# Fourier branch of a two-layer diffusion backbone: the short transform's PSUM tile moves to the single ring, and 16 convolution taps per layer move from the branch's end into the gates

## The chip, the core and the metric

The kernel runs on one core of one Trainium2 chip. Its engines are TensorE (PE; its weight loads PEld), VectorE (DVE), ScalarE (ACT), GpSimd (POOL) and SyncE (SP), which issues the transfers. The metric is the device time of one execution in microseconds. The kernel before takes 2163.43 us, the median of three runs (2162.35 to 2165.26).

## The reference

Two layers are applied to 640 tokens (512 of a sample, 128 of a prompt) of width 1024. What matters here are the three parallel mixers of a layer, their gates and the merge:

```python
f_in, conv_in, q_lat, kv_lat, k_rope = jnp.split(u, cuts, axis=-1)
y_f = fourier_mix(f_in) @ W['w_fourier'][l]
y_c = conv_module(conv_in, ...)      # gate, 31 taps, layer_norm, silu, matmul
y_a = block_attention(q, k, v) @ W['w_mla_out'][l]
gates = jax.nn.sigmoid(h @ W['w_gate'][l] + W['b_gate'][l])
gf, gc, ga = jnp.split(gates, N_BRANCH, axis=-1)
x = x + g1 * ((gf * y_f + gc * y_c + ga * y_a) @ W['w_out'][l])

def fourier_mix(f_in):               # (B, L, 512), 4 groups of 128 channels
    z = f_in.astype(jnp.float32).reshape(B, L, F_GROUPS, F_GROUP_W)
    y = jnp.fft.fft2(z, axes=(1, 3), norm='ortho').real
    return y.reshape(B, L, F_W).astype(f_in.dtype)

def layer_norm(x, g, b):             # over the 512 convolution channels
    mu = jnp.mean(xf, axis=-1, keepdims=True)
    var = jnp.mean(jnp.square(xf - mu), axis=-1, keepdims=True)
    y = (xf - mu) * lax.rsqrt(var + EPS)
```

The Fourier transform runs over the tokens too: over 512 for the sample, over 128 for the prompt.

## The kernel before

Channels lie on the partitions and the 640 tokens along the free dimension, in two halves of 320. Every large product is made of three (L621, `mm3`): a weight is cut into a high part `whi` (ScalarE, L182) and a low part `wlo` (VectorE, L183), the activation likewise (`split`, L666 and L667), and high by high, high by low and low by high are added up in PSUM. Weights come in one planned stream of DMAs (`Stream`), are split two pieces ahead of their use, and sit in small rings of buffers.

PSUM has two rings: `psum()` (`ps`) gives three tiles of two banks each, `psum1()` (`ps1`) two tiles of one bank. The next user of a tile waits on TensorE until the last readers of its former content are done.

After the attention, `mixers` runs: the Fourier branch (`fourier`), eight gates `gf` (each `gate`: eight blocks of the gate's weights, 48 matmuls, then four blocks of the branch's output weights, 24 matmuls), eight gates `ga` for the attention, eight `gc` for the convolution, and the output projection. In `fourier` four products give `fT` (L1265), five channel transforms of 128 tokens each give `Th`, `Tl` and `tp` (L1284), the long transform over 512 tokens fills two `ps` tiles (L1313 to L1320), and for each of two pairs of groups the short one over 128 tokens fills `pq` (L1326 to L1328): its cosine part in the first bank, its sine part in the second (column 512). ScalarE copies the cosine part (L1334), VectorE takes difference and sum with the sine part (L1335, L1336), ScalarE mirrors the halves (L1338, L1339) and the results are split into `yh` and `yl`, which the gates `gf` read.

The convolution is a generator, `conv_gen`, that other code steps through `fill(n)`. Its 124 taps (L1105, L1107) are VectorE work, one step each. Step 125 adds the four accumulators up (`cs`, L1116), sums them over the channels with a matmul by ones (`colsum`, L491) and takes the mean on ScalarE (L1120). Step 126 subtracts the mean (L1123), squares and adds (`sumsq`, L500 to L504, result `sqa`), sums `sqa` over the channels with L491 again, and forms the inverse deviation (L454 to L458). Steps 127 to 130 finish one channel block each. The order in the program is the order of these calls; the framework then moves single instructions forward on an engine where they are ready, so that taps of two blocks alternate on VectorE. Each engine works through its own list in order.

Of the kernel before, what the change touches and what calls it, by code (L numbers as in the profile page):

```python
# [14 lines left out]
ALU = mybir.AluOpType  # L15
# [190 lines left out]
class Kern:  # L206
# [936 lines left out]
    def mixers(self, l, h, oT, xsrc, up, upp, uctx, wctx):  # L1143
        nc, tc = self.nc, self.tc
# [3 lines left out]
        with self.rpool("mix") as mp, ExitStack() as ctx:  # L1148
# [3 lines left out]
            def b640(n):  # L1152
                return [r640("b", F32R, 16) for _ in range(n)]
# [5 lines left out]
            def fill(n):  # L1159
                for _ in range(n):  # L1160
                    next(bg, None)
# [4 lines left out]
            with self.rpool("m1") as lp:  # L1166
                ad = self.ada_gate() if l == 0 else iter(())
                m1 = [lp.tile([128, NT], F32, tag="m1", name=self.nm("m1"), bufs=8) for _ in range(8)]
                for m in range(8):
                    self.gate(l, r640, "gf", "wf", m, hh, hl, yh, yl, bgh[:, m : m + 1], m1[m])  # L1170
                    next(ad, None)
                    fill(9)
                next(ad, None)
                oh, ol = b640(4), b640(4)
                for k in range(4):
                    self.split(oh[k], ol[k], oT[k])
                x = []
                for k in range(KT):
                    t = self.xt()
                    nc.sync.dma_start(out=t, in_=xsrc[:, k, :])  # L1180
                    x.append(t)
                self.x = x
                for m in range(8):
                    t = self.gate(l, r640, "ga", "wa", m, hh, hl, oh, ol, bgh[:, 16 + m : 17 + m], None)
                    nc.vector.tensor_tensor(m1[m], m1[m], t, op=ALU.add)
                    fill(7)
                for _ in bg:
                    pass
                ctx.close()
                uctx.close()  # L1190
                actx = ExitStack()
                ad = iter(())
                if l == 0:
                    ad = self.ada_dots(actx.enter_context(self.lpool("ad")), [(0, 24, 40)])
                with self.rpool("mm") as mm:
                    mh, ml = [], []
                    for m in range(8):
                        mh += b640(1)
                        ml.append(mm.tile([128, NT], F32R, tag="ml", name=self.nm("ml"), bufs=8))
                        t = self.gate(l, r640, "gc", "wc", m, hh, hl, U[0], U[1], bgh[:, 8 + m : 9 + m], None)  # L1200
                        nc.vector.tensor_tensor(m1[m], m1[m], t, op=ALU.add)
                        r = self.split(mh[m], ml[m], m1[m])
                        with tc.issue_after(r.ins):
                            for _ in range(1 + m % 2):
                                next(ad, None)
                    g1h = self.lay.tile([128, 8, 2], F32, tag="g1h", name=self.nm("g1h"))
                    nc.vector.tensor_scalar(g1h, self.mods[l][:, 16:24, :], 0.5, None, op0=ALU.mult)
                    segs = (((0, 0, 320, 0),), ((0, 320, 192, 0), (192, 512, 128, 1)))
                    cols = ((0, 320), (320, 640))
                    nm = self.norm_gen(  # L1210
                        l, 2, lambda n: lp.tile([128, NT], F32, tag="m1", name=self.nm(n), bufs=8)
                    )
                    next(nm)
                    for m in range(6):
                        p = self.psum()
                        q = (p[:, 0:320], p[:, 512:832])
                        self.gemm(p, l, "wo", m, mh, ml)
                        for b in range(2):
                            r = self.addx(m, q[b], g1h, segs[b])
                        with tc.issue_after(r.ins):  # L1220
                            next(ad, None)
                        if m == 3:
                            for _ in ad:
                                pass
                            actx.close()
                            wx = wctx.enter_context(self.lpool("wx"))
                        next(nm)
                    w = [[self.st.get("wo", l, m, h) for h in range(2)] for m in (6, 7)]

                    def run(i, k):  # L1230
                        c = slice((k % 4) * 128, (k % 4 + 1) * 128)
                        wh, wl = w[i][k // 4]
                        return lambda oo: self.mm3(oo, wh[:, c], wl[:, c], mh[k], ml[k], k == 0, k == 7)

                    self.st.spare["upa", l, 1] = (wx, "f")
                    return self.last_pair(nm, [[run(i, k) for k in range(8)] for i in range(2)], cols, segs, g1h, 6)
# [24 lines left out]
    def fourier(self, l, fo, hh, hl, yh, yl, r640, fill):  # L1261
        nc = self.nc
        fT = []
        for m in range(4):
            p = self.psum()  # L1265
            self.gemm(p, l, "f", m, hh, hl)
            t = fo.tile([128, NT], F32, tag="fT", name=self.nm("fT"), bufs=4)
            nc.scalar.copy(self.halves(t), self.v2(p))
            fT.append(t)
            fill(5)  # L1270
        Th, Tl = [], []

        def tview(t):
# [6 lines left out]
        for i in range(5):  # L1280
            p = self.psum()
            for g in range(4):
                o = (g // 2) * 512 + (g % 2) * 130
# [3 lines left out]
            if i < 4:  # L1287
                a = fo.tile([128, 520], F32R, tag="Th", name=self.nm("Th"), bufs=4)
                b = fo.tile([128, 520], F32R, tag="Tl", name=self.nm("Tl"), bufs=4)
# [3 lines left out]
            else:  # L1293
                tp = fo.tile([128, 520], F32, tag="tp", name=self.nm("tp"))
                nc.scalar.copy(tview(tp), pview(p))

        def wcols(t, pr, kind):
            o, n = {"P": (0, 128), "Q": (128, 128), "K": (256, 2)}[kind]
            return t[:, pr * 260 + o : pr * 260 + o + n]

        ps = [self.psum() for _ in range(2)]
# [19 lines left out]
                                    ps[pr][:, 0:258], lhsT=wcols(a[i], pr, "P"), rhs=b[:, r], start=first, stop=fin  # L1321
                                )
        for pr in range(2):
            pq = self.psum()
            Cp, Sp = self.tb[:, 130:196], self.tb[:, 196:262]
            nc.tensor.matmul(pq[:, 0:66], lhsT=wcols(tp, pr, "P"), rhs=Cp, start=True, stop=True)  # L1326
            nc.tensor.matmul(pq[:, 512:578], lhsT=wcols(tp, pr, "Q"), rhs=Sp, start=True, stop=True)
            nc.tensor.matmul(pq[0:2, 512:578], lhsT=wcols(tp, pr, "K"), rhs=Cp, start=False, stop=True, skip_group_check=True)  # L1328
            ym = self.xt(name="ym")
            yp = self.xt(name="yp")  # L1330
            for src, o, L in ((ps[pr], 0, 512), (pq, 512, 128)):
                hw = L // 2 + 1
                pc = r640("gt", F32, 2)
                nc.scalar.copy(pc[:, 0:hw], src[:, 0:hw])  # L1334
                nc.vector.tensor_tensor(ym[:, o : o + hw], pc[:, 0:hw], src[:, 512 : 512 + hw], op=ALU.subtract)  # L1335
                nc.vector.tensor_tensor(yp[:, o : o + hw], pc[:, 0:hw], src[:, 512 : 512 + hw], op=ALU.add)  # L1336
                for d, s in ((ym, yp), (yp, ym)):
                    nc.scalar.copy(d[:, o + hw : o + L], s[:, o + hw - 2 : o : -1])  # L1338
                    nc.scalar.copy(d[0:2, o + hw : o + L], d[0:2, o + hw - 2 : o : -1])  # L1339
            self.split(yh[2 * pr], yl[2 * pr], ym)  # L1340
            self.split(yh[2 * pr + 1], yl[2 * pr + 1], yp)
            fill(6)
    def ffn(self, l, h2):
        nc = self.nc
        hh, hl = h2
# [281 lines left out]
```

## Time and profile before

| | |
|---|---|
| Median of three runs | 2163.43 us |
| The profiled execution | 2164.37 us |
| Its span, first to last instruction | 2162.6 us |
| Mean granted clock of TensorE | 0.996 |
| TensorE, VectorE, ScalarE busy | 2119.4, 1499.8, 916.0 us |

The profile names each instruction by its line and by what it writes and reads (`out<-in`). A row of the timeline gives its start, its time and in brackets how long the engine stood idle before it and what it waited for by the profile. Matmuls overlap: a row's time is longer than the step from one to the next. A wait for several engines is put down to the one that came last by the profile, and that can be the wrong one. The clock of TensorE has two levels, 1.2 and 2.4 GHz, shown as 0.50 and 1.00.

### The profile page before, as it was taken

The numbers are of one execution on the slowest core, as the hardware profiler recorded it, in microseconds if no ns is written. First come the engines' busy times: TensorE is split into PE (matmuls) and PEld (weight loads), VectorE is DVE, ScalarE is ACT, GpSimd is POOL, SyncE is SP. The second block draws the span as 40 slices with busy tenths as digits, with TensorE's granted clock in tenths as the row PEclk, the third lists the DMA queues.
The fourth block names the chain that finished last, engine by engine and source line by source line (L and its number), as shares of the span: only waits on it lengthen the run. The fifth ranks groups of instructions, "written<-read, shape, count | busy, mean of one in ns | idle before, by whom it ended". The sixth has DMA issues, their size and how long they took to land.

```text
span 2162.6 us, 35613 instructions
## 1 busy us (share of the span) xinstructions
PE 2119.4 (98%) x14380; PEld 2046.3 (95%) x14380; DVE 1499.8 (69%) x2585; ACT 916.0 (42%) x1786; POOL 115.7 (5%) x243
## 2 busy tenths in 40 slices
PE   6999999999999999999999999999999999999999
PEld 4988899999999999999988889999999999999998
DVE  6675699757778868977877767996544864455454
ACT  4654342353345424514456553424432643343242
POOL 0242100000000000000002421000000000000000
PEclk9999999999999999999999999999999999999999
DMA  7211033324424344444431101222222222222222
GB/s 279 64 50 30 30 104 124 110 98 147 156 88 136 128 156 137 152 151 132 154 104 61 44 21 50 93 93 73 78 75 78 69 76 72 79 79 69 78 74 79
DMA packets 61797, 209.32 MB, mean 97 GB/s; under 512 B 7488, under 2 KB 8512, under 8 KB 61376
## 3 DMA queue, kind: packets, MB, share of 16 engines
q1 hardware_dynamic: 61632, 207.04, 29.2%
q8 instruction: 113, 1.85, 0.4%
q14 instruction: 52, 0.43, 0.1%
HBM read 201.47 MB, written 5.54 MB: 96 GB/s over the span
## 4 chain that ended last, share of the span: by engine, by line
PE 64%; DVE 3%; ACT 1%; POOL 1%; issue 0%; DMA 0%; DVEq 0%; ACTq 0%; POOLq 0%
PE ps L621 60%; PE ps L953 1%; PE ps L1007 1%; DVE wlo L183 1%; PE ps L990 1%; PE ps L827 0%; DVE hl L552 0%; PE ps L936 0%; DVE nt L548 0%; DVE cacc L1107 0%; PE ps L847 0%; ACT P L941 0%; ACT whi L182 0%; PE ps L994 0%; PE ps L593 0%
## 5 line engine op out<-in xcount | busy, mean ns | idle before, releaser
L182 ACT CAST whi<-raw 128x512 fp32r<-128x512 f32 (+3 forms) x546 | 332.4, 611 | 872.2 <-PE ps L621 807.3
L621 PE MATMUL ps<-hh,whi 128*128 128x320 f32 x2720 | 641.2, 313 | 10.5 <-ACT hh L551 3.7
L621 PE MATMUL ps<-hh,wlo 128*128 128x320 f32 x2720 | 640.5, 311 | 4.4 <-DVE wlo L183 4.4
L621 PE MATMUL ps<-hl,whi 128*128 128x320 f32 x2720 | 640.1, 311 | 0.8 <-DVE hl L552 0.4
L183 DVE TENSOR_TENSOR wlo<-raw,whi 128x512 fp32r<-128x512 f32 (+3 forms) x544 | 370.6, 688 | 235.2 <-ACT whi L182 231.9
L621 PEld LDWEIGHTS ps<-hh,whi 128*128 128x128 f32 x2720 | 457.8, 189 | 19.5 <-ACT hh L551 5.6
L621 PEld LDWEIGHTS ps<-hh,wlo 128*128 128x128 f32 x2720 | 460.4, 189 | 6.4 <-DVE wlo L183 5.9
L621 PEld LDWEIGHTS ps<-hl,whi 128*128 128x128 f32 x2720 | 461.2, 189 | 5.3 <-DVE hl L552 3.7
L621 PE MATMUL ps<-b,whi 128*128 128x320 f32 x1024 | 207.1, 308 | 0.0
L1107 DVE SCALAR_TENSOR_TENSOR cacc<-up,cdwh,cacc 128x656 f32<-128x656 f32 x240 | 206.4, 901 | 0.7
L1381 DVE SCALAR_TENSOR_TENSOR ft<-fr,pf,ft 128x641 f32<-128x641 f32 x176 | 155.3, 885 | 57.4 <-ACT ft L1377 56.2
L322 DVE SCALAR_TENSOR_TENSOR junk<-adw,cb 128x1024 f32<-128x1024 f32 x144 | 175.7, 1220 | 1.0 <-DMA adw<-in_adt 0.9
L621 PE MATMUL ps<-al,whi 128*128 128x320 f32 x704 | 165.3, 310 | 0.0
L621 PE MATMUL ps<-ah,whi 128*128 128x320 f32 x704 | 165.2, 309 | 0.1
L621 PEld LDWEIGHTS ps<-b,whi 128*128 128x128 f32 x1024 | 164.8, 188 | 0.0
L621 PE MATMUL ps<-ah,wlo 128*128 128x320 f32 x704 | 164.2, 309 | 0.0
L621 PE MATMUL ps<-b,wlo 128*128 128x320 f32 x640 | 151.3, 309 | 0.0
L621 PEld LDWEIGHTS ps<-ah,whi 128*128 128x128 f32 x704 | 118.8, 188 | 1.6 <-ACT ah L666 1.6
L621 PEld LDWEIGHTS ps<-al,whi 128*128 128x128 f32 x704 | 118.5, 188 | 0.6
L621 PEld LDWEIGHTS ps<-ah,wlo 128*128 128x128 f32 x704 | 118.6, 188 | 0.1
L1241 DVE SCALAR_TENSOR_TENSOR x<-ps,g2h,x 128x320 f32<-128x320 f32 (+1 forms) x144 | 54.8, 435 | 83.9 <-PE ps L621 83.7
L621 PEld LDWEIGHTS ps<-b,wlo 128*128 128x128 f32 x640 | 108.2, 188 | 0.2
(272 smaller groups left out, 2258.9 us busy)
## 6 DMA issues: line engine op xcount, KB each, us to landing
raw<-in_ws SPq DMA_DIRECT2D x247, 512.0 KB, 3.4
adw<-in_adt SPq DMA_DIRECT2D x72, 512.0 KB, 4.2
ad<-in_ad SPq DMA_DIRECT2D x16, 512.0 KB, 9.9
raw<-in_ws SPq DMA_DIRECT2D x20, 384.0 KB, 3.1
x<-in_xT SPq DMA_DIRECT2D x16, 320.0 KB, 4.0
xd<-x SPq DMA_DIRECT2D x8, 320.0 KB, 2.6
x<-xd SPq DMA_DIRECT2D x8, 320.0 KB, 3.1
out_yT<-x SPq DMA_DIRECT2D x8, 320.0 KB, 2.2
```

Of the source, the lines that this page charges most:

```text
L182: nc.scalar.copy(h, src)
L183: nc.vector.tensor_tensor(l, src, h.bitcast(F32), op=ALU.subtract)
L322: nc.vector.scalar_tensor_tensor(junk, w[at(n)], 0.5, cb[:, v], op0=ALU.mult, op1=ALU.mult, accum_out=md[:, i, v : v + 1])
L621: nc.tensor.matmul(o, lhsT=w, rhs=x[:, lo:hi], start=(start and i == 0), stop=(stop and i == 2))
L953: nc.tensor.matmul(p[:, c * 512 : c * 512 + 320], lhsT=a[:, i * 128 : (i + 1) * 128], rhs=b[:, c * 320 : c * 320 + 320], start=(n == 0), s ...
L990: nc.tensor.transpose(p[:, b * 128 : (b + 1) * 128], src[:, b * 128 : (b + 1) * 128], self.ident)
L1007: nc.tensor.matmul(p[n * 64 : (n + 1) * 64, 0:256], lhsT=vv[b][:, 2 * j + n, :], rhs=pts[j, h][:, b, n, :], start=(b == 0), stop=(b == 4),)
L1107: nc.vector.scalar_tensor_tensor(a, up[m][:, t : t + UCW], ws, a, op0=ALU.mult, op1=ALU.add)
L1241: r = self.nc.vector.scalar_tensor_tensor(xs, p[:, pc : pc + n], g[:, m, v : v + 1], xs, op0=ALU.mult, op1=ALU.add)
L1381: nc.vector.scalar_tensor_tensor(t[:, c], raw[:, o : o + 641], w[:, 3 * jj + tap : 3 * jj + tap + 1], t[:, c], op0=ALU.mult, op1=ALU.add,)
```

## The change

Two things are edited. The short transform's tile `pq` comes from `psum1()`, so both parts lie in one bank, the sine part from column 256. And `fill` is called with other counts: in `fourier` behind the fourth product 0 instead of 5 and behind the third 4; behind the pairs 0 and 2 instead of 6 and 6; in the gates `ga` 8 instead of 7.

```diff
@@ mixers, the gates ga
                     nc.vector.tensor_tensor(m1[m], m1[m], t, op=ALU.add)
-                    fill(7)
+                    fill(8)
@@ fourier
             fT.append(t)
-            fill(5)
+            fill((5, 5, 4, 0)[m])
...
         for pr in range(2):
-            pq = self.psum()
+            pq = self.psum1()
             Cp, Sp = self.tb[:, 130:196], self.tb[:, 196:262]
             nc.tensor.matmul(pq[:, 0:66], lhsT=wcols(tp, pr, "P"), rhs=Cp, start=True, stop=True)
-            nc.tensor.matmul(pq[:, 512:578], lhsT=wcols(tp, pr, "Q"), rhs=Sp, start=True, stop=True)
-            nc.tensor.matmul(pq[0:2, 512:578], lhsT=wcols(tp, pr, "K"), rhs=Cp, start=False, stop=True, skip_group_check=True)
+            nc.tensor.matmul(pq[:, 256:322], lhsT=wcols(tp, pr, "Q"), rhs=Sp, start=True, stop=True)
+            nc.tensor.matmul(pq[0:2, 256:322], lhsT=wcols(tp, pr, "K"), rhs=Cp, start=False, stop=True, skip_group_check=True)
...
-            for src, o, L in ((ps[pr], 0, 512), (pq, 512, 128)):
+            for src, o, L, b in ((ps[pr], 0, 512, 512), (pq, 512, 128, 256)):
...
-                nc.vector.tensor_tensor(ym[:, o : o + hw], pc[:, 0:hw], src[:, 512 : 512 + hw], op=ALU.subtract)
-                nc.vector.tensor_tensor(yp[:, o : o + hw], pc[:, 0:hw], src[:, 512 : 512 + hw], op=ALU.add)
+                nc.vector.tensor_tensor(ym[:, o : o + hw], pc[:, 0:hw], src[:, b : b + hw], op=ALU.subtract)
+                nc.vector.tensor_tensor(yp[:, o : o + hw], pc[:, 0:hw], src[:, b : b + hw], op=ALU.add)
...
-            fill(6)
+            fill((0, 2)[pr])
```

The first place is TensorE at the end of layer 1's Fourier branch, where the first gate follows the short transform. The name before the first number is the ring, the first number the tile. Before:

```order
L1326 MATMUL ps_1626_14673<-tb_103,tp_1623_14577 128x66
L1327 MATMUL ps_1626_14673<-tb_103,tp_1623_14577 128x66
L1328 MATMUL ps_1626_14673<-tb_103,tp_1623_14577 2x66
L1326 MATMUL ps_1631_14705<-tb_103,tp_1623_14577 128x66
L1327 MATMUL ps_1631_14705<-tb_103,tp_1623_14577 128x66
L1328 MATMUL ps_1631_14705<-tb_103,tp_1623_14577 2x66
L621 MATMUL ps_1646_14750<-hh_1087_11430,whi330_14627 128x320 x2
L621 MATMUL ps_1646_14750<-hl_1095_11438,whi330_14627 128x320 x2
```

In the changed kernel:

```order
L1326 MATMUL ps1_1626_14667<-tb_103,tp_1623_14571 128x66
L1327 MATMUL ps1_1626_14667<-tb_103,tp_1623_14571 128x66
L1328 MATMUL ps1_1626_14667<-tb_103,tp_1623_14571 2x66
L1326 MATMUL ps1_1631_14693<-tb_103,tp_1623_14571 128x66
L1327 MATMUL ps1_1631_14693<-tb_103,tp_1623_14571 128x66
L1328 MATMUL ps1_1631_14693<-tb_103,tp_1623_14571 2x66
L621 MATMUL ps_1645_14733<-hh_1087_11430,whi330_14621 128x320 x2
L621 MATMUL ps_1645_14733<-hl_1095_11438,whi330_14621 128x320 x2
```

The instructions and their sequence are the same. The short transform's two tiles are of the ring `ps1`, and in the ring `ps` the gate's tile (1645) follows those of the long transform (1624 and 1625, on L1313 to L1320).

The second place is TensorE in layer 1's gates `ga`, at the two column sums of the convolution. Before, with the gate between them cut out:

```order
L621 MATMUL ps_15853<-b_15563,wlo_15794 128x320 x2
L491 MATMUL ps_15894<-cs_15890,ones 128x328 x2
L621 MATMUL ps_15899<-hh_11430,whi_15823 128x320 x2
...
L621 MATMUL ps_15960<-b_15563,wlo_15903 128x320 x2
L491 MATMUL ps_16008<-sqa_15997,ones 128x328 x2
L621 MATMUL ps_16057<-hh_11430,whi_15930 128x320 x2
```

In the changed kernel:

```order
L621 MATMUL ps_16041<-b_15550,whi_15981 128x320 x2
L621 MATMUL ps_16041<-b_15546,wlo_15982 128x320 x2
L491 MATMUL ps_16080<-cs_16076,ones 128x328 x2
L491 MATMUL ps_16100<-sqa_16089,ones 128x328 x2
L621 MATMUL ps_16131<-hh_11430,whi_16011 128x320 x2
L621 MATMUL ps_16131<-hl_11438,whi_16011 128x320 x2
```

The two sums stood before and behind the fourth gate; now they stand one behind the other, behind the fifth gate. Layer 0 has the same.

The third place is VectorE at those sums, from the merge of the gate's result (L1185) on. Before:

```order
L1185 TENSOR_TENSOR m_1640_14744<-m_1640_14744,gt_15851 128x640
L1123 TENSOR_TENSOR cacc_14332<-cacc_14332,cmu_15897 128x656
L1123 TENSOR_TENSOR cacc_14736<-cacc_14736,cmu_15897 128x656
L1123 TENSOR_TENSOR cacc_15148<-cacc_15148,cmu_15897 128x656
L1123 TENSOR_TENSOR cacc_15455<-cacc_15455,cmu_15897 128x656
L183 TENSOR_TENSOR wlo_15964<-raw_15961,whi_15963 128x512
L504 TENSOR_TENSOR sqa_15997<-sqa_15997,sq_15999 128x656
L504 TENSOR_TENSOR sqa_15997<-sqa_15997,sq_16002 128x656
L504 TENSOR_TENSOR sqa_15997<-sqa_15997,sq_16005 128x656
L183 TENSOR_TENSOR wlo_16059<-raw_15961,whi_16058 128x512
```

In the changed kernel:

```order
L1185 TENSOR_TENSOR m_1641_14729<-m_1641_14729,gt_16039 128x640
L1123 TENSOR_TENSOR cacc_14332<-cacc_14332,cmu_16083 128x656
L1123 TENSOR_TENSOR cacc_14932<-cacc_14932,cmu_16083 128x656
L1123 TENSOR_TENSOR cacc_15332<-cacc_15332,cmu_16083 128x656
L1123 TENSOR_TENSOR cacc_15672<-cacc_15672,cmu_16083 128x656
L504 TENSOR_TENSOR sqa_16089<-sqa_16089,sq_16091 128x656
L504 TENSOR_TENSOR sqa_16089<-sqa_16089,sq_16094 128x656
L504 TENSOR_TENSOR sqa_16089<-sqa_16089,sq_16097 128x656
L456 SCALAR_TENSOR_TENSOR rt_16105<-rs_16104 128x656
L457 SCALAR_TENSOR_TENSOR rt_16105<-ps_16100,rt_16105 128x656
L458 SCALAR_TENSOR_TENSOR rs_16104<-rt_16105,rs_16104 128x656
```

The weight split between the subtractions (L1123) and the additions (L504) has gone, as have a split and the next gate's product (L1256) and merge (L1185) between the additions and the work on the inverse deviation (L456 to L458).

## Rows read from the trace of the kernel before

**Rows 1.** Page, part 1: busy us (share of the span) and instructions of each engine.

```profile
PE 2119.4 (98%) x14380; PEld 2046.3 (95%) x14380; DVE 1499.8 (69%) x2585; ACT 916.0 (42%) x1786; POOL 115.7 (5%) x243
```

**Rows 2.** Waits of TensorE: who waits, for whom: us, times, longest.

```profile
PE ps L537 <- DVE sqa L504: 13.7, 1, 13.7
PE ps L621 <- DVE wlo L183: 4.4, 4, 3.6
...
PE ps L621 <- ACT yp L1338: 1.7, 1, 1.7
```

**Rows 3.** Timeline, TensorE, layer 1's Fourier end: start, us, operation, xcount [idle <- releaser].

```profile
1372.67 0.28 PE L1328 MATMUL ps<-tb,tp 128*2 128x66 f32 x2
1374.60 0.87 PE L621 MATMUL ps<-hh,whi 128*128 128x320 f32 x2 [1.65 <-ACT yp L1338]
```

**Rows 4.** Timeline, VectorE, the same place.

```profile
1368.02 0.69 DVE L183 TENSOR_TENSOR wlo<-raw,whi 128x512 fp32r<-128x512 f32 x1
...
1371.88 0.90 DVE L1107 SCALAR_TENSOR_TENSOR cacc<-up,cdwh,cacc 128x656 f32<-128x656 f32 x1
1372.69 0.69 DVE L183 TENSOR_TENSOR wlo<-raw,whi 128x512 fp32r<-128x512 f32 x1
1373.29 0.90 DVE L1107 SCALAR_TENSOR_TENSOR cacc<-up,cdwh,cacc 128x656 f32<-128x656 f32 x1
...
1374.23 0.22 DVE L1336 TENSOR_TENSOR yp<-gt,ps 128x65 f32<-128x65 f32 x1
```

**Rows 5.** Windows: stretch, us, busy PE, PEld, DVE, ACT, POOL, granted clock, DMA, GB/s.

```profile
1374.60:1377.90 3.30, 3.30 (x12) 3.30 (x13) 3.22 (x6) 3.02 (x11) 0.00 (x0) 0.50 0.47 155
1377.90:1385.00 7.10, 7.10 (x50) 7.10 (x50) 5.55 (x10) 4.44 (x10) 0.00 (x0) 1.00 0.52 151
27.80:33.00 5.20, 5.16 (x19) 5.03 (x20) 5.20 (x14) 5.20 (x12) 0.00 (x0) 0.50 1.03 412
666.20:671.20 5.00, 4.93 (x18) 4.93 (x19) 5.00 (x10) 0.73 (x1) 0.00 (x0) 0.50 0.60 199
1101.30:1106.00 4.70, 3.32 (x14) 2.07 (x14) 4.70 (x12) 2.35 (x6) 0.00 (x0) 1.00 0.52 170
```

**Rows 6.** Timeline, TensorE, the first gate of layer 0.

```profile
304.00 0.53 PE L621 MATMUL ps<-hh,whi 128*128 128x320 f32 x2 [0.24 <-DVE yp L1336]
```

**Rows 7.** Timeline, TensorE, layer 1's column sums.

```profile
1492.28 1.26 PE L491 MATMUL ps<-cs,ones 128*128 128x328 f32 x4
1493.14 0.70 PE L621 MATMUL ps<-hh,whi 128*128 128x320 f32 x2
...
1503.93 1.27 PE L491 MATMUL ps<-sqa,ones 128*128 128x328 f32 x4
```

**Rows 8.** Timeline, VectorE and then ScalarE, between the column sums.

```profile
1494.63 3.09 DVE L1123 TENSOR_TENSOR cacc<-cacc,cmu 128x656 f32<-128x656 f32 x4
1497.64 0.68 DVE L183 TENSOR_TENSOR wlo<-raw,whi 128x512 fp32r<-128x512 f32 x1
1498.24 2.73 DVE L504 TENSOR_TENSOR sqa<-sqa,sq 128x656 f32<-128x656 f32 x3
...
1493.59 0.72 ACT L1120 ACTIVATE cmu<-ps 128x656 f32<-128x656 f32 x1 [0.78 <-PE ps L491]
```

**Rows 9.** Timeline, VectorE, the end of the taps in layer 1.

```profile
1475.07 0.84 DVE L1116 TENSOR_TENSOR cs<-cs,cacc 128x656 f32<-128x656 f32 x1
```

**Rows 10.** Timeline, TensorE, three other waits (start, layer 0 FFN, layer 1).

```profile
27.84 0.64 PE L621 MATMUL ps<-hh,whi 128*128 128x320 f32 x1 [3.22 <-ACT whi L182]
666.27 0.90 PE L621 MATMUL ps<-hh,wlo 128*128 128x320 f32 x2 [3.65 <-DVE wlo L183]
1101.37 0.56 PE L621 MATMUL ps<-hh,whi 128*128 128x320 f32 x2 [1.77 <-ACT hh L551]
```

**Rows 11.** Line L491, both layers: ns min/median/max, first and last start.

```profile
L491 PE MATMUL ps<-cs,ones x8: 437/438/439, 426.1 to 1493.1; 128*128 128x328 f32 x8
L491 PE MATMUL ps<-sqa,ones x8: 437/438/440, 437.7 to 1504.8; 128*128 128x328 f32 x8
```

## The prediction

> **What bounds the kernel now.** I read the page first, then the list of waits of TensorE, then the timelines of the two stages that the change touches, and last the granted clock in windows. The page says that TensorE is busy for 98% of the span, VectorE for 69%, ScalarE for 42% [rows 1]. So an edit is worth what it takes from, or adds to, the few places where TensorE has nothing to issue. The list of waits has few of them: 13.7 us at the start of the program, 4.4 us for the low parts of weights, and 1.7 us behind a line of the Fourier branch, L1338 [rows 2]. The reader should note which of these the change can reach: only the last.
>
> That wait stands at the end of layer 1's Fourier branch. TensorE ends the second short transform (L1328) at 1372.95 and starts the first gate at 1374.60, after 1.65 us of idle time [rows 3]. The row names ScalarE as releaser, but the gate needs a free PSUM tile of the ring of three, and all three are held by the long and the short transforms. The one that comes free in time is the first short transform's: its last reader is VectorE's second 65-wide operation, which ends at 1374.45, and the gate starts 0.15 us behind it. Before that operation stand two convolution taps and a weight split: 1371.88, 1372.69, 1373.29 [rows 4]. Then the gate runs slowly: 12 matmuls from 1374.60 to 1377.90 at a granted clock of 0.50, which is the 1.2 GHz level of the two; from 1377.90 it is 1.00, 2.4 GHz [rows 5]. In layer 0 the same place costs 0.24 us, with no fall of the clock [rows 6].
>
> The second place is inside the gates of the third kind (`ga`). There the convolution's LayerNorm puts two column sums on TensorE, L491: `cs` (for the mean) and `sqa` (for the variance). Between them TensorE does one whole gate, `cs` at 1492.28, the gate from 1493.14, `sqa` at 1503.93, and it waits for neither [rows 7]. What lies between the two sums on the other engines is a chain: ScalarE takes the mean at 1493.59, VectorE subtracts it four times from 1494.63, ScalarE squares, and VectorE adds three times from 1498.24 to 1500.97 [rows 8]. The gate hides all of that.
>
> **The change, part by part.** *The short transform in the single ring.* The first gate's tile then comes free long before, and the 65-wide operations hold it no more. The second half of its weights is split at 1368.02, long before [rows 4]. What is late next is the gate's second half, which reads the Fourier result: the gate starts at about 1372.95, and a full gate of 72 matmuls takes 10.8 us (1493.14 to 1503.93 [rows 7]), 0.15 each; its first 48 take 7.2 us and the next 18 another 2.7, so the last of the four results is wanted at about 1382.9. By the new order of ScalarE its cast stands behind the gate's tanh, which can start at 1380.2. I allow 0.7 us each for the tanh, the cast and VectorE's split (the rows of such size, 0.69 for a split of 512 columns and 0.72 for the mean [rows 4, 8]): 1382.3. That fits by some 0.6 us. I take the wait as gone: 1.65 us. With it goes the slow stretch: 3.30 us [rows 5] for 12 matmuls that take 1.8 at 0.15, so 1.5 us. Layer 0 gives 0.24 [rows 6]. Together 3.4 us gained; bounds 0 (something else holds the gate) and 3.4 (no more stands there to be gained).
>
> *The taps.* Each layer moves 16 of its 124 tap steps out of the Fourier branch. The generator has 130 steps. Before, 32 are taken in the Fourier branch, 72 in the first gates, so after the `ga` gates of 7 the count is 111, 118, 125, 130. Step 125 holds `cs`, step 126 `sqa`: they fall on both sides of the fourth gate. Now it is 16 + 72 = 88, and by eights 96, 104, 112, 120, 128: steps 125 and 126 are taken in one call, after the fifth `ga` gate. The listing of TensorE's order says the same: `sqa` directly behind `cs`, in both layers. The taps themselves I cost at 0: VectorE ended the last of them and the sum (L1116) at 1475.91, 16 us before TensorE wanted it [rows 9]; the new place is two gates, 21 us, later. Counting the new order's instructions between gates at the durations of the rows (a tap 0.8, a split 0.6 [rows 4]) gives at most 11.6 us of VectorE for a gate of 10.8, against 11.5 before, so without that cover it would be 1 us at most.
>
> *The pair of sums, a new wait.* TensorE must now stand from `cs` until `sqa`'s operand is there, with all later work queued behind it. The chain in the rows: the first subtraction starts 2.35 us after `cs` starts (1492.28 to 1494.63), four take 3.01 (to 1497.64), three additions 2.73 [rows 7, 8]. The weight split that stood between them (0.60) is no longer there by the new order. So `sqa` can start 2.35 + 3.01 + 2.73 + 0.1 = 8.2 us after `cs`; today the instruction behind `cs` starts 0.86 us after it (1493.14). The loss is 7.3 us per layer (6.9 of it will be seen as idle time, since the rows let `cs` end at 1493.54). Bounds: 6.6 if the additions overlap the subtractions by one, 7.9 if a split still stands between. I take 7.3: 14.6 us for two layers. Layer 0 has the same spacing, 11.6 us from `cs` to `sqa` [rows 11], so the two layers are taken alike. Behind the waiting `sqa` stand the next gate and all that follows on TensorE; ScalarE's casts and VectorE's splits of later weights wait in turn for the places that TensorE frees, so all of them shift by the same amount and none becomes late by it. By the new order ScalarE loads two function tables fewer in each layer; nothing waited for them, so 0.
>
> *The clock after it.* The nearest rows: after an idle time of 3.65 us at 666.27, 5.0 us ran at 0.50; after 3.22 us at 27.84, 5.2 us did; after 1.65 us, 3.3; but after 1.77 us at 1101.37 the clock stayed at 1.00 [rows 5, 10]. Half of such a stretch is lost: 2.5, 2.6, 1.6 or 0. A wait of 7 us is nearest to the first two: 2.5 us per layer, 5.0 in all; bounds 0 and 2.6 per layer.
>
> The Trainium skill, "TensorE: Matmul & The Clock Gate", section "A second HAM failure mode: psum-queue depth-cycling", says that idling a little between groups of matmuls while the PSUM places go round brings the clock down, with the throttling paid each time. Layer 1's wait of 1.65 us bears that out and the wait of 1.77 us at 1101.37 does not. By that rule both column-sum waits are throttled, which is the sum below; by the row at 1101.37 alone the sum would be 5.0 us less, which is the second rival.
>
> The sum: 14.6 + 5.0 - 3.4 = 16.2 us on the profiled execution's 2164.37 us (its span of 2162.6 and 1.8 around it), 2180.6. That execution lies 0.94 above the median of 2163.43, so against the median I predict 2179.6.
>
> **The rivals.** First, on the other side: TensorE is not held, because it takes the next gate's matmuls past the waiting `sqa`. Then only the Fourier gain is left, 2163.4 - 3.4 = 2160.0, faster. It decides as soon as TensorE gets one gate ahead of a waiting instruction. Against it: at 666.27 one product of a weight's low part held TensorE for 3.65 us, and not one product behind it went ahead [rows 10]. I give it 3%.
>
> Second: the waits come, but the clock stays up, as at 1101.37. 2179.6 - 5.0 = 2174.6. For it speaks one row, against it three. 8%.
>
> Third, the change does not do what it says at the Fourier end: the gate finds another late operand (the fourth result with its 0.6 us of margin, or a weight), TensorE idles about as long as now and the clock falls again. Then the 3.4 us are not gained: 2183.0. For it speaks how full VectorE is there (no idle time in [rows 4]); against it that fewer taps stand in the chain. 12%.
>
> **How the numbers follow.** The forecast has 77%. Its own spread comes from the bounds: 6.6 to 7.9 and 0 to 2.6 per layer, gains of 0 to 3.4. The far ends are 2163.4 + 13.2 + 0 - 3.4 = 2173.2 and 2163.4 + 15.8 + 5.2 = 2184.4; the range of 2174.4 to 2183.3 leaves out the first rival and the corners. A measurement of this kernel tells a difference of about 0.2%, 4.3 us. All cases but the first rival are at least 9 us slower, so slower 0.96, faster 0.03, same 0.01.
>
> **What would show it.** In the profile after: two rows of L491 `sqa` with about 6.9 us of idle time before them, released by VectorE's `sqa` (L504); a granted clock near 0.50 for some 5 us behind each; no wait at the first gate in layer 1 and a clock of 1.00 there; no other new wait of TensorE above 1 us. The prediction is wrong if `sqa` starts within 2 us of `cs`, if the clock behind it is 1.00, or if TensorE still idles over 1 us between L1328 and L621.

## The result, and the profile after

The changed kernel takes 2180.06 us (median of 6 runs, 2179.18 to 2180.80); the kernel before, run beside it, 2163.08 us (6 runs, 2161.46 to 2165.26). The ratio is 1.0078, 95% interval 1.0066 to 1.0090: slower by 17.0 us (14.3 to 19.5). The forecast was 2179.6, between 2174.4 and 2183.3. The profiled execution took 2180.09 us, its span 2178.3; that is 15.7 us more than the profiled execution before, on both counts.

Part 1 of the page after, as in [rows 1]:

```profile
PE 2123.6 (97%) x14380; PEld 2048.2 (94%) x14380; DVE 1501.0 (69%) x2585; ACT 911.9 (42%) x1782; POOL 116.1 (5%) x243
```

TensorE has as many instructions as before and 4.2 us more busy time, so some of them ran slower. Its idle time, span less busy time, is 54.7 us against 43.2: 11.5 us more. Those two numbers are the whole 15.7 us of the profiled pair. Where the idle time sits, TensorE's list of waits says, as in [rows 2]:

```profile
PE ps L537 <- DVE sqa L504: 13.9, 1, 13.9
PE ps L491 <- DVE sqa L504: 13.7, 2, 6.9
PE ps L621 <- DVE wlo L183: 4.2, 3, 3.8
```

The second line is new: two waits of 6.9 us each, in the column sum, for the sum of squares. The line of L1338 is gone. The timelines of layer 1's column sums, first TensorE, then VectorE, then ScalarE, correspond to [rows 7, 8]:

```profile
1520.38 1.26 PE L491 MATMUL ps<-cs,ones 128*128 128x328 f32 x4
1528.51 2.56 PE L491 MATMUL ps<-sqa,ones 128*128 128x328 f32 x4 [6.87 <-DVE sqa L504]
1530.38 1.22 PE L621 MATMUL ps<-hh,whi 128*128 128x320 f32 x2
...
1538.33 0.75 PE L621 MATMUL ps<-b,whi 128*128 128x320 f32 x4
```
```profile
1522.72 3.09 DVE L1123 TENSOR_TENSOR cacc<-cacc,cmu 128x656 f32<-128x656 f32 x4
1525.73 2.73 DVE L504 TENSOR_TENSOR sqa<-sqa,sq 128x656 f32<-128x656 f32 x3
```
```profile
1521.68 0.72 ACT L1120 ACTIVATE cmu<-ps 128x656 f32<-128x656 f32 x1 [0.78 <-PE ps L491]
```

The gate that stood between the two sums is gone, and TensorE stands through mean, subtractions and additions; each of them takes as long as before. The second sum itself takes 2.56 us instead of 1.27, and so do the first matmuls behind it. The windows show why; the columns are those of [rows 5], the number behind the last bracket is the granted clock (0.50 is the 1.2 GHz level, 1.00 the 2.4 GHz level):

```profile
456.30:459.90 3.60, 3.53 (x9) 2.68 (x10) 0.01 (x1) 0.91 (x2) 0.00 (x0) 0.50 0.00 0
1528.50:1531.80 3.30, 3.29 (x8) 2.46 (x9) 0.00 (x0) 0.70 (x1) 0.00 (x0) 0.51 0.00 0
1531.80:1540.00 8.20, 8.20 (x58) 8.20 (x57) 7.12 (x9) 5.89 (x9) 0.00 (x0) 1.00 0.00 0
676.20:681.70 5.50, 5.42 (x20) 5.42 (x21) 5.50 (x10) 0.94 (x2) 0.00 (x0) 0.50 0.53 182
1111.70:1115.20 3.50, 3.50 (x12) 2.77 (x12) 3.50 (x9) 1.46 (x4) 0.00 (x0) 0.53 0.49 190
1383.00:1390.00 7.00, 7.00 (x49) 6.99 (x48) 6.92 (x14) 5.41 (x20) 0.00 (x0) 1.00 0.45 136
```

Behind each column-sum wait TensorE runs for some 3.5 us at 0.50. The clock had already fallen inside the wait. In layer 0 the wait lasts from 449.50 to 456.37, and of two windows in it, neither with a matmul, the first is at 1.00 and the second at 0.50:

```profile
450.00:453.10 3.10, 0.00 (x0) 0.00 (x0) 3.10 (x5) 1.90 (x4) 0.00 (x0) 1.00 0.00 0
453.20:456.30 3.10, 0.00 (x0) 0.00 (x0) 2.89 (x4) 2.53 (x3) 0.00 (x0) 0.50 0.00 0
```

The whole stretch at 0.50 lasts 6.8 us in either layer (453.15 to 459.98 and 1524.93 to 1531.76); 3.2 and 3.6 us of it lie in the wait, where there is no matmul to slow down.

The last row of the windows further up is layer 1's first gate, now at 1.00 throughout. Its start, as in [rows 3], follows the short transforms without a gap:

```profile
1382.81 0.28 PE L1328 MATMUL ps<-tb,tp 128*2 128x66 f32 x2
1383.01 0.56 PE L621 MATMUL ps<-hh,whi 128*128 128x320 f32 x2
```

The last sum of the taps, as [rows 9], for both layers (ns min/median/max, first and last start):

```profile
L1116 DVE TENSOR_TENSOR cs<-cs,cacc x2: 836/839/842, 409.4 to 1485.5; 128x656 f32<-128x656 f32 x2
```

It ends at 1486.3, and TensorE wants it at 1520.38: the taps have 34 us to spare.

Where the 15.7 us arise can be read by matching the two traces: the n-th matmul of one with the n-th of the other. After starts later than before by 0.4 us ahead of layer 0's Fourier end, 1.0 behind it, 9.9 behind layer 0's sums, 10.3 ahead of layer 1's Fourier end, 7.0 behind it, and 15.7 from layer 1's sums to the end. At layer 1's Fourier end, for instance, L1328 starts at 1372.67 [rows 3] and 1382.81, and the first gate's first `b` matmul, before and after, at

```profile
1383.21 0.75 PE L621 MATMUL ps<-b,whi 128*128 128x320 f32 x4
1390.17 0.75 PE L621 MATMUL ps<-b,whi 128*128 128x320 f32 x4
```

So the sums cost 8.9 and 8.7 us, layer 1's Fourier end gives 3.3, and layer 0's costs 0.6.

### The profile page after: what moved, and what is told of

It is laid out like the page before. It is cut to its first block, busy times and chain, and to the rows that moved or that the text cites. A ratio compares the mean times of both kernels' runs of the same rounds, so it can differ in the third digit from the quotient of the medians.

```text
span 2178.3 us, 35610 instructions
## 1 busy us (share of the span) xinstructions
PE 2123.6 (97%) x14380; PEld 2048.2 (94%) x14380; DVE 1501.0 (69%) x2585; ACT 911.9 (42%) x1782; POOL 116.1 (5%) x243
## 4 chain that ended last, share of the span: by engine, by line
PE 64%; DVE 3%; ACT 1%; POOL 1%; issue 0%; DMA 0%; DVEq 0%; ACTq 0%; POOLq 0%
PE ps L621 59%; PE ps L953 1%; PE ps L1007 1%; PE ps L990 1%; DVE wlo L183 1%; PE ps L827 0%; DVE hl L552 0%; PE ps L936 0%; DVE nt L548 0%; PE ps L847 0%; ACT P L941 0%; PE ps L994 0%; PE ps L593 0%; POOL kn L876 0%; DMA adw<-in_adt 0%
```

## The experiments

The theory: the changed kernel loses by the two column sums falling into one call of the generator, 7.3 us of standing and a low clock behind it in each layer, and gains a few us at the Fourier end by the single ring. The main rivals: the short transform's new tile, or the taps' new places, cause the loss; the low clock costs nothing; TensorE waits for something other than the chain of the sums.

**The pair taken apart (e1_pair_apart).** The changed kernel with

```diff
-                    fill(8)
+                    fill((8, 8, 8, 8, 5, 8, 8, 8)[m])
```

> The changed kernel with the fifth gate's step count cut from 8 to 5 (counts 96, 104, 112, 120, 125, 130), so that a whole gate stands between the two column sums again; all else as in the change. Theory 1 (the pair of sums is the whole loss): no wait at L491, TensorE's clock stays at 1.00, and the Fourier gain of 3.4 us is left: about 2159.7 us where before is 2163.1. Rival (the loss comes from the taps being done later, or from the one-bank tile): about 2180 us as in the changed kernel.

Measured: 2160.91 us (11 runs, 2160.27 to 2162.08) against 2162.86 for the kernel before (27 runs, which e1 to e4 share); ratio 0.9992, 0.9983 to 1.0001. TensorE's timeline in layer 1:

```profile
1510.97 1.26 PE L491 MATMUL ps<-cs,ones 128*128 128x328 f32 x4
1511.82 0.71 PE L621 MATMUL ps<-hh,whi 128*128 128x320 f32 x2
...
1522.64 1.27 PE L491 MATMUL ps<-sqa,ones 128*128 128x328 f32 x4
```

With a gate between the sums again there is no wait and no slow matmul, and the whole loss is gone; the time is 1.2 us above the 2159.7 of theory 1, which lies within the interval. Everything else of the change is in this kernel, so the whole of the loss hangs on which steps share a call.

**The pair joined in the kernel before (e2_pair_joined).** The kernel before with

```diff
-                    fill(7)
+                    fill((7, 7, 6, 7, 7, 7, 7, 7)[m])
```

> The kernel before with one number changed: the third ga gate takes 6 steps and not 7 (counts 111, 118, 124, 130), so that both column sums are taken in one call behind the fourth gate. Theory 1: two waits of 6.9 us of idle time (7.3 lost) and some 1.7 us each at the low clock, 18 us: about 2181 us. Rival: about 2163 us, since no tap is moved out of the Fourier branch and its tile stays in the ring of three.

Measured: 2183.38 us (4 runs, 2181.66 to 2184.01), ratio 1.0093, 1.0079 to 1.0107. TensorE in layer 1, at the Fourier end and at the sums:

```profile
1382.86 0.87 PE L621 MATMUL ps<-hh,whi 128*128 128x320 f32 x2 [1.65 <-ACT yp L1338]
...
1511.11 1.27 PE L491 MATMUL ps<-cs,ones 128*128 128x328 f32 x4
1519.60 2.56 PE L491 MATMUL ps<-sqa,ones 128*128 128x328 f32 x4 [7.22 <-DVE sqa L504]
```

One step fewer in one call out of eight makes a kernel with nothing else of the change slower by 20.5 us, 2.5 more than theory 1 said. In the profiled pair, matched as above, the two sums cost 8.9 and 9.0 us, about its 18; the medians are further apart because this profiled execution lies 1.7 us below its median and the one before 1.5 above. The kernel keeps the wait at the Fourier end and lies 3.3 us above the changed kernel, which is free of it (2183.38 to 2180.06; the two were run on different occasions).

**The ring alone (e3_ring_only)** and **the fills alone, pair apart (e4_fills_only).** The first is the kernel before with the short transform's tile from the single ring (its second half at column 256, as in the change), the second the kernel before with the new fills, and the pair apart as in e1:

```diff
-            pq = self.psum()
+            pq = self.psum1()
```
```diff
-            fill(5)
+            fill((5, 5, 4, 0)[m])
-            fill(6)
+            fill((0, 2)[pr])
-                    fill(7)
+                    fill((8, 8, 8, 8, 5, 8, 8, 8)[m])
```

> The short transform's tile in the single ring, all step counts as before. Theory 2 (the wait at layer 1's first gate is for a free tile of the ring of three): the gate starts at once, no fall of the clock; the taps still in VectorE's list may make the fourth Fourier result late by up to 0.9 us per layer: 2159.7 to 2161.5 us. Rival (the wait is VectorE's queue of taps, wherever the tile lies): the wait moves to the Fourier result, 1.5 us or more of idle time with the low clock behind it, about 2163 us.

> The other part alone: the step counts of the change in the Fourier branch (5, 5, 4, 0 and 0, 2) with the ga counts that keep the sums apart (8, 8, 8, 8, 5), and the tile in the ring of three. Theory 2: the first gate still waits for the short transform's last reader, which now has no two taps ahead of it but still ScalarE's copies; the wait of 1.65 us in layer 1 shrinks to 0.5 to 1.2 us and does not vanish: 2161 to 2163 us, and the low clock behind it decides. Rival: the wait is gone as in the change, 2159.7 us.

Measured: e3 2160.90 us (11 runs, 2159.90 to 2162.02), ratio 0.9990, 0.9982 to 0.9999; e4 2164.11 us (11 runs, 2162.62 to 2165.01), ratio 1.0005, 0.9997 to 1.0014. The first gate of layer 1 behind the short transform (TensorE's timeline) and the clock behind it (windows), in e3 and then in e4:

```profile
1372.94 0.56 PE L621 MATMUL ps<-hh,whi 128*128 128x320 f32 x2
```
```profile
1372.90:1380.00 7.10, 7.10 (x50) 7.06 (x49) 7.02 (x15) 5.00 (x17) 0.00 (x0) 1.00 0.43 126
```
```profile
1372.83 0.53 PE L621 MATMUL ps<-hh,whi 128*128 128x320 f32 x2 [1.44 <-ACT yp L1338]
```
```profile
1374.50:1376.00 1.50, 1.50 (x7) 1.50 (x7) 1.50 (x3) 1.35 (x5) 0.00 (x0) 0.50 0.00 0
```

The ring takes away the wait and the low clock by itself, within the range expected of e3. Moving taps out of the Fourier branch leaves 1.44 of the 1.65 us, and e4 misses both its numbers (0.5 to 1.2 us, 2161 to 2163 us). VectorE's timeline in e4 says why: two weight splits and a tap still stand ahead of the first short transform's last reader,

```profile
1370.32 1.28 DVE L183 TENSOR_TENSOR wlo<-raw,whi 128x512 fp32r<-128x512 f32 x2
1371.53 0.89 DVE L1107 SCALAR_TENSOR_TENSOR cacc<-up,cdwh,cacc 128x656 f32<-128x656 f32 x1
...
1372.47 0.21 DVE L1336 TENSOR_TENSOR yp<-gt,ps 128x65 f32<-128x65 f32 x1
```

and the gate starts 0.15 us behind that reader (1372.68 to 1372.83), as it does before. So the gain is the ring's: 2.0 us in e3 against the kernel before, 3.2 us in e1 against e4, which differ in the ring alone. Taking fewer taps in the Fourier branch gives nothing that can be measured.

**The wait filled (e5_wait_filled).** The changed kernel with matmuls between the sums:

```diff
         self.colsum(p, s, UCW // 2)
+        q = self.psum1()
+        for _ in range(14):
+            nc.tensor.matmul(q[:, 0:328], lhsT=self.ones, rhs=s[:, 0:328], start=True, stop=True)
```

> The changed kernel, but between the two column sums of the convolution's LayerNorm TensorE does 14 further matmuls of the same size as a column sum's (128x328, 0.437 us each in the profile), into a PSUM bank that nobody reads: 6.1 us of work in a wait of 6.9 us. They are extra work; nothing is left out. Theory (the pair costs its wait and, on top, half of a low-clock stretch of 3.4 us behind it): the column sum of squares starts as late as before, 8.1 us after the first sum, idle time before it falls to about 0.8 us, the granted clock behind it stays at 1.00, and the time falls by 1.7 us for each layer, 3.4 in all, from 2180.1 to about 2176.7. Rival (the low clock behind the wait costs nothing, since later work has slack): 2180.

Measured: 2177.01 us (5 runs, 2176.80 to 2177.46), 3.1 us less than the changed kernel's 2180.06; ratio to the kernel before (2163.20, 9 runs, which e5 and e6 share) 1.0062, 1.0049 to 1.0076. TensorE's timeline in layer 1, and a window with its clock:

```profile
1518.49 1.26 PE L491 MATMUL ps<-cs,ones 128*128 128x328 f32 x4
1519.59 7.89 PE L1121 MATMUL ps<-cs,ones 128*128 128x328 f32 x28
1527.31 1.27 PE L491 MATMUL ps<-sqa,ones 128*128 128x328 f32 x4
...
1535.47 0.75 PE L621 MATMUL ps<-b,whi 128*128 128x320 f32 x4
```
```profile
1527.30:1535.00 7.70, 7.70 (x50) 7.34 (x49) 4.62 (x6) 4.11 (x5) 0.00 (x0) 1.00 0.01 2
```

The size of the filling was off: each matmul of this type shows as two in the trace (x28), and together they took 7.7 us, not 6.1, so the second sum started 8.82 us after the first instead of 8.13. Work was added and the sum came later, yet the kernel is faster. From the second sum to the next gate's first `b` matmul it takes 8.16 us here (1527.31 to 1535.47) and 9.82 in the changed kernel (1528.51 to 1538.33): 1.7 us of clock in layer 1, and in layer 0, by the same rows there, 8.18 against 10.00, 1.8. The low clock costs time, 3.5 us in all, and the rival falls. Less the 0.69 us by which each second sum is later, the two places give 2.1 us of the 3.1; the rest lies elsewhere, so that the time met its 2176.7 is partly chance.

**A shorter chain (e6_two_squares).** The changed kernel with

```diff
-        sq = self.sumsq(tmp, acc)
+        sq = self.sumsq(tmp, acc[:2])
```

> The changed kernel, but the sum of squares of the convolution's LayerNorm takes two of its four channel groups (two squares on ScalarE and two additions on VectorE, 0.91 us each, are left out, so the variance is another). Theory (TensorE stands for exactly the chain mean, subtractions, additions): the wait falls by 2 x 0.91 = 1.8 us in each layer, from 6.9 to 5.1, and the time by 3.6 us, from 2180.1 to about 2176.5. Rival (TensorE waits for something else that only ends at the same time, a weight or a PSUM bank): the wait stays at 6.9 us and the time at 2180, at most 0.5 us less.

Measured: 2176.76 us (5 runs, 2176.05 to 2177.38), 3.3 us less; ratio to the kernel before 1.0061, 1.0048 to 1.0073. TensorE's wait in layer 1, VectorE's one addition, and windows: the end of layer 0's wait, then behind the waits of layer 0 and layer 1:

```profile
1523.73 2.56 PE L491 MATMUL ps<-sqa,ones 128*128 128x328 f32 x4 [4.98 <-DVE sqa L504]
```
```profile
1522.84 0.83 DVE L504 TENSOR_TENSOR sqa<-sqa,sq 128x656 f32<-128x656 f32 x1
```
```profile
451.30:453.20 1.90, 0.00 (x0) 0.00 (x0) 1.90 (x3) 1.71 (x2) 0.00 (x0) 0.50 0.00 0
453.20:458.00 4.80, 4.74 (x13) 3.89 (x14) 0.53 (x2) 1.56 (x2) 0.00 (x0) 0.50 0.00 0
1523.70:1529.90 6.20, 6.17 (x19) 5.34 (x20) 1.82 (x3) 1.56 (x2) 0.00 (x0) 0.50 0.00 0
```

The wait fell by 1.89 us, the two additions (0.91 us each) and no more: TensorE stands for just this chain. So the wait is settled. That the time came out as expected is partly chance: the low stretches behind the shorter waits are longer, 4.8 and 6.2 us against 3.6 and 3.3. The stretches themselves are as long as in the changed kernel, 6.8 us (451.30 to 458.13 and 1523.09 to 1529.91), but only 2.0 and 0.6 us of them lie in the shorter waits. From the second sum to the first `b` matmul it takes 10.55 and 11.16 us, 1.9 more in all than in the changed kernel, so these two places give 3.8 - 1.9 = 1.9 us of the 3.3; the other 1.4 lie elsewhere. In the profiled pair, matched, elsewhere means 1.2 us gained at the start, 1.3 near 674 us and 1.0 lost near 1110 us.

**The two kernels profiled once more (e7_before_again, e8_after_again).** Nothing is edited.

> The kernel before, unchanged, profiled once more. Theory (whether the granted clock falls behind a wait of TensorE, and for how long, differs from one execution to the next): behind the wait of 1.77 us near 1101 us, where the clock stayed at 1.00 in the first profile, it may be 0.50 for about 3.5 us, and behind the wait of 3.65 us near 666 us the low stretch may be 3.5 instead of 5.2 us. Rival (it is fixed by the order of work in the kernel): both places read as in the first profile, 1.00 and 5.2 us. Time 2163 by both.

> The changed kernel, unchanged, profiled once more. Theory (each wait's low-clock stretch is drawn anew in each execution): the stretches behind the two column-sum waits, 3.4 us each in the first profile, read between 2.2 and 5.2 us, the wait itself again 6.9 us; the clock behind the wait of 1.77 us near 1111 us may stay at 1.00. Rival (fixed by the kernel): 3.4 us each and a low clock near 1111 as in the first profile. Time 2180 by both.

Measured: 2162.48 and 2178.97 us (one run each). Windows behind the waits of 27, 665 and 1099 us in the kernel before, and behind both column-sum waits and the waits of 675 and 1110 us in the changed one:

```profile
27.60:31.00 3.40, 3.40 (x13) 3.19 (x14) 3.40 (x10) 3.40 (x9) 0.00 (x0) 0.52 1.03 412
666.00:669.40 3.40, 3.40 (x15) 3.40 (x15) 3.40 (x7) 0.73 (x1) 0.00 (x0) 0.50 0.68 237
1099.60:1104.30 4.70, 3.39 (x15) 2.15 (x15) 4.70 (x12) 2.36 (x5) 0.00 (x0) 1.00 0.54 183
```
```profile
455.40:459.00 3.60, 3.56 (x9) 2.72 (x10) 0.00 (x0) 0.93 (x2) 0.00 (x0) 0.51 0.00 0
1527.40:1530.80 3.40, 3.39 (x8) 2.55 (x9) 0.00 (x0) 0.80 (x1) 0.00 (x0) 0.51 0.00 0
675.20:680.90 5.70, 5.68 (x21) 5.69 (x22) 5.70 (x9) 1.21 (x2) 0.00 (x0) 0.51 0.53 176
1110.50:1115.00 4.50, 4.22 (x14) 3.19 (x14) 4.50 (x11) 2.16 (x5) 0.00 (x0) 0.62 0.52 182
```

Neither theory holds in full. In the kernel before the low stretches at 27 and 665 us lasted 3.4 us this time, against 5.2 and 5.0 in [rows 5], so they differ between executions of one kernel; the span was 1.9 us shorter. The wait of 1.77 us kept its clock both times in the kernel before and lost it both times in the changed one, and the stretches behind the column sums repeat to 0.1 us. The low clock near the wait of 1.77 us doesn't belong to the change: the clock falls at it, or up to 2.4 us behind it, in e2 to e6 as well, and not in e1, which has nearly all of the change. Nor does it cost anything in the changed kernel. The next wait of its kind, before and after, is

```profile
1105.27 0.56 PE L621 MATMUL ps<-hh,whi 128*128 128x320 f32 x2 [0.81 <-ACT hh L551]
1115.47 0.56 PE L621 MATMUL ps<-hh,whi 128*128 128x320 f32 x2 [0.22 <-ACT hh L551]
```

3.90 us behind 1101.37 [rows 10] and 3.89 behind 1111.58: the slow matmuls only fill a wait that was there anyway.

## Why the prediction was right

The direction, the place and the time came out: 2180.06 against 2179.6. By its steps:

- **The pair of sums.** Predicted 8.2 us from `cs` to `sqa`, 6.9 us of it idle, 7.3 lost per layer. Measured 8.13 and 6.87 in both layers, 8.13 - 0.86 = 7.27 lost. Undoing it takes the whole loss away (e1), doing it alone makes the loss (e2), and shortening its chain shortens the wait by as much (e6). The count of the generator's steps and the durations of [rows 7, 8] were enough. The first rival, TensorE going past the waiting sum, did not occur; nor did the second, a clock that stays up.
- **The clock behind it.** The wait was throttled in both layers, but "2.5 us per layer, 5.0 in all" was mis-sized: 1.8 and 1.7, 3.5 in all (e5). The step took what runs slowly behind a wait from the waits nearest in length, 3.65 and 3.22 us, and expected some 5 us; behind the 6.87 us it was 3.3 and 3.6, because half of the 6.8 us at 0.50 passed inside the longer wait. The Trainium skill, "TensorE: Matmul & The Clock Gate", section "A second HAM failure mode: psum-queue depth-cycling", says of another kernel that short idling between groups of matmuls, when it is frequent enough, makes the clock go down and up. It doesn't speak of a single wait. At the column sums the clock did fall (0.50 behind all four waits of the two profiles after); at the wait of 1.77 us it fell in the changed kernel and not in the one before.
- **The Fourier end.** Predicted 3.4 us gained: the wait of 1.65 us and the low clock behind it are gone in layer 1, and the ring alone does it (e3). In time the term measures 2.0 us (e3), 3.2 us (e1 against e4) and 3.3 us (e2 against the changed kernel); the first two are of runs on one chip. The interval of e3 reaches from 0.2 to 3.9, so 3.4 is not excluded. Matched against the profile before, TensorE gains 3.3 us at layer 1's Fourier end in the changed kernel, in e1 and in e3, and loses 0.6 at layer 0's, where the step counted 0.24 gained: 2.7 in all. What costs the 0.6 was not followed up. The third rival did not occur.
- **What is late next there.** I had the fourth Fourier result ready 0.6 us before TensorE wants it. The estimate moved into the changed kernel (its gate starts 10.06 us later) is ready at 1392.4, wanted at 1393.0. In fact VectorE's split of it ended at 1393.7:

```profile
1392.91 0.82 DVE L667 TENSOR_TENSOR b<-yp,b 128x640 fp32r<-128x640 f32 x1
```
```profile
1393.99 0.31 PE L621 MATMUL ps<-hh,whi 128*128 128x320 f32 x1
1394.13 0.45 PE L621 MATMUL ps<-b,whi 128*128 128x320 f32 x2
```

By my deadline that would have been a wait of 0.8 us. The order of TensorE's instructions puts matmuls of the next gate (`hh`, `hl`) ahead of the last `b` ones, which I had not looked for, and they cover it: right in its result, not in its reason.
- **The taps.** 0 predicted; e4's 1.3 us above the kernel before is within its interval (-0.6 to 3.0).

By the matched traces the sums cost 17.6 us where 14.6 + 5.0 = 19.6 were predicted, the Fourier ends give 2.7 where 3.4 were, and 0.8 us arise elsewhere (0.4 ahead of layer 0's Fourier end, 0.3 near 676 us), less than the 1.9 by which two executions of the kernel before differ. That is the 15.7 us of the profiled pair. The medians' 17.0 is 1.3 more because the profiled execution before lies 1.3 us above the median of the six runs of its kernel (2164.37 to 2163.08). That 16.2 came so near was partly luck: a term for the sums 2.0 us too large, 1.5 of it the clock, stood against a Fourier gain 0.7 too large and 0.8 that the sum doesn't hold.

No version here beats the kernel before by more than 0.1%: e1 and e3 take 2160.9 us both.

## What to carry to other kernels

When side work is fed into a main stream by a count of steps, work out in which call each step that uses the main engine falls: two dependent steps in one call have nothing between them, and the engine stands for the whole chain of the others. A change of a count by one moves such a pair together or apart, and here it decided 17 us where the edit it came with was worth 2 to 3. To see it before running, look for a pair in the order of instructions and read the chain between them from the trace.

## What the runs showed of the hardware

- The low clock behind a wait doesn't grow with the wait: 6.87 us of idle time were followed by 3.3 to 3.6 us at 0.50 (four waits), 4.98 us by 4.8 and 6.2 (e6), 3.5 to 4.1 us near 670 us by 3.0 to 5.7 (all ten profiles). At the column sums the clock was down for 6.8 us each time (after, e2, e6, e8) from a point inside the wait, so the longer wait left less of it for matmuls.
- A low clock can be free: behind the wait of 1.77 us the changed kernel ran 3.4 us at 0.50 and reached the next matmul that has to wait after 3.89 us, against 3.90 at full clock before. It isn't always so: in e3 6.8 us at 0.50 near the same place cost 1.0 us, matched against the kernel before.
- A wait can cost less filled than empty: 7.7 us of matmuls that nobody needs in place of 6.87 us of idle time made the kernel 3.1 us faster, though the sum behind them started 0.69 us later in each layer (e5).
- One kernel's low stretches can differ from one execution to the next, 5.0 and 5.2 us against 3.4 at the same two places. Matched, 0.7 us of the 1.9 by which its two spans differ arise at each of them.
